# Weight units of 2048 columns split in one piece instead of two

## The chip, the cores and the metric

The kernel runs on one core of a Trainium2 chip. The metric is the device time of one execution in microseconds; three runs of the kernel before gave 905.27, 903.74 and 903.62, with a median of 903.74.

The engines of the core work side by side, each through its own list of instructions in order: TensorE (PE) multiplies matrices, ScalarE (ACT) and VectorE (DVE) work on elements, GpSimd (POOL) does a few odd things, and SyncE (SP) issues the transfers that bring the weights from HBM.

## The reference

Two layers of a hybrid encoder in float32, on 256 tokens of width 1024. One layer is, cut to what matters here:

```python
u = rms_norm(h, g_mix_pre)
gq, gk, gv, gg, ra_f, ra_b, aq, ak, av, gate_a, gate_b = split(u @ w_in)
a = (rms_norm(gla(forward) + gla(backward)) * silu(gg)) @ w_o_gla
b = gqa_attention(rope(rms_norm(aq)), rope(rms_norm(ak)), av) @ w_o_attn
h = h + rms_norm((sigmoid(gate_a) * a + sigmoid(gate_b) * b) @ w_out)
gate, up = split(rms_norm(h) @ w_ffn_in)
h = h + rms_norm((silu(gate) * up) @ w_ffn_out)
h = h + rms_norm(sigmoid(h @ w_ple_gate) * (p[i] @ w_ple_proj))
```

Nearly all the work is in the products with weights: `w_in`, `w_o_gla`, `w_o_attn`, `w_out`, `w_ffn_in`, `w_ffn_out`, `w_ple_gate` and `w_ple_proj`, each of which is read once per layer.

## The kernel before

**Products in three passes.** A float32 product is made of products of fp32r numbers. Each operand is split into a high part, the value rounded to fp32r, and a low part, the difference between the value and its high part. A product is then high by high, plus high by low, plus low by high. For the weights, `split` (L134 to L136) makes the high part `wh` with a copy on ACT and the low part `wl` with a subtract on DVE. The subtract reads what the copy wrote. `passes` (L116 to L124) issues the matmuls of a quarter of a product: for the four rows of 128 that a unit holds, first the eight matmuls that read only `wh` and then the four that read `wl` (with `fresh` both parts come earlier). The matmuls themselves are recorded at L108 (the helper `mm`) and L124 (`passes`).

**Units of weights.** All weights come as a stream of 176 units in a fixed order, listed by `plan` (L206 to L234). A unit is a 128x2048 block of float32 in SBUF: four blocks of 128 rows by 512 columns of a weight matrix, say. Eight units, those that also hold the decay ranks of `w_in`, are 2112 columns wide. `Load` and `Stream` (L236 to L367) carry them. `Stream.start` issues a unit's transfers on SP into a raw tile; there are three raw tiles. `Stream.fill` takes the next unit as soon as fewer than four are held. It calls `put`, which allocates the pair `wh` and `wl` (four of each) and cuts the unit into pieces; `fill` then calls `split` on each piece and asks for the next transfer. A raw tile comes free when the last subtract that reads it is done. `take` hands the oldest split unit to a product, and `done` gives its buffers back when the product is issued.

**Sums of units.** Part of the products over 2x2 blocks are done with seven block products instead of eight, on sums and differences of blocks. `Stream.step` (L324 to L346) forms the sums of weights with adds of 128x2048 on DVE (L328, L331, L334, L339) and puts each sum through `made`, which calls `put` and `split` too. In these the raw tiles are lent `wh` and `wl` tiles (`lent`) or larger scratch tiles (`big`).

**Order of the work.** A planner orders the instructions of each engine when the program is built, by priorities and its own estimate of times. What is within a block of high priority goes ahead when it is ready; `issue_after` pins one instruction behind another. On the chip each engine follows that order. `self.cast` and `self.last[n]` keep the instructions of the last piece of a unit, so that other instructions can be pinned behind it (`behind`, L357).

**Stages.** A layer runs through the keys and values of the GLA branch and the attention (`gqk`, `kv`, `rq`, `v`, `at`), the out-gate of the GLA branch (`gg`), the gates and merges of the branches (`gate`, `merge`), `wout`, the FFN (`ffnin`) and the input embedding (`ple`). Names of tiles in the profile carry the layer and the stage, so that `acc_0gate` is an accumulator in PSUM of the gate stage of layer 0.

**Transposes and gates.** The outputs of one product become the left operand of the next after a transpose. At the end of the FFN's first product they are transposed on PE (`transpose_in`, matmuls with the identity at L452) and split in turn, elsewhere by a DMA (`turn_out`, `take_in`, L458 to L484, with copies on ACT at L468 and L478). The FFN's gate is a silu on ACT (L1655) and a product on DVE (`vmul`, L129), which give the tile `t_0ffnin`.

Of the kernel before, what the change touches and what calls it, by code (L numbers as in the profile page):

```python
# [62 lines left out]
def trunk_kernel(ctx: ExitStack, tc: tile.TileContext, a: dict, out: bass.AP):  # L63
# [21 lines left out]
    def nm(s):  # L85
        uid[0] += 1
        return f"{s}_{part[0]}_{uid[0]}"
# [161 lines left out]
    class Stream:  # L249
# [51 lines left out]
                        on("dma", nc.sync.dma_start, dst, src)  # L301
                x.n = sum(math.prod(dst.shape[1:]) for dst, _ in moves)

        def put(self, x, parts=2):

            wh = wp.tile([P, UNIT], F32R, tag="wh", name=nm("wh"))
            wl = wp.tile([P, UNIT], F32R, tag="wl", name=nm("wl"))
            self.ready.append((wh, wl))
            self.held += 1
            cuts = [slice(j * x.n // parts, (j + 1) * x.n // parts) for j in range(parts)]  # L310
            return [(wh[:, c], wl[:, c], x.raw[:, c]) for c in cuts]
# [1494 lines left out]
```

## Time and profile before

| | |
|---|---|
| median of 3 runs | 903.74 us |
| lowest and highest run | 903.62 and 905.27 us |
| span of the profiled execution | 903.0 us |
| PE busy | 892.9 us in 4431 matmuls |
| DVE busy | 790.0 us in 1021 instructions |
| ACT busy | 641.4 us in 1035 instructions |
| read from and written to HBM | 169.50 and 3.15 MB |

The span is the time from the first to the last record of the profiled execution; the median of the runs is 0.7 us above it. Busy times are sums over an engine's instructions, with the profile's modelled ends for PE, so that an engine whose busy time is 99% of the span has nearly always an instruction under way. A row of the timeline gives the start in us, the length, the engine with the line of the kernel, the operation, what it writes and reads, the shape and how many such instructions are put together; in brackets stands the idle time before it and what ended that. A row of the groups gives the count, the busy time, the mean length of one in ns, and the idle time ahead of the group's instructions.

### The profile page before, as it was taken

How to read it: one execution, taken by the hardware profiler on the slowest of the kernel's cores; microseconds unless marked ns; L12 is line 12 of the kernel's file. 1: busy time of each engine (PE TensorE's matmuls, PEld its weight loads, DVE VectorE, ACT ScalarE, POOL GpSimd, SP SyncE). 2: the span in 40 equal slices, each digit the busy share in tenths (PEclk: the TensorE clock that was granted, in tenths of full speed). 3: DMA queues.
4: the chain of work that ended last, by engine and by line, in shares of the span. 5: the costliest groups of instructions: out<-in, count | busy, mean ns of one | idle time of the engine just before them, and what ended most of it. 6: DMA issues, size and time to landing. Idle time of an engine off the chain costs nothing.

```text
span 903.0 us, 12130 instructions
## 1 busy us (share of the span) xinstructions
PE 892.9 (99%) x4431; PEld 759.0 (84%) x4431; DVE 790.0 (87%) x1021; ACT 641.4 (71%) x1035; POOL 104.4 (12%) x157
## 2 busy tenths in 40 slices
PE   9999999999999999999999999999999999999996
PEld 8888888888888888888898888888888888888885
DVE  7899989997679999999779799899985799999984
ACT  6669769965468787766676697698645696967653
POOL 3800221000310000000234003210001100000001
PEclk9999999999999999999999999999999999999998
DMA  8764448469296695947476544473683966867441
GB/s 276 256 206 132 155 157 220 124 220 351 66 325 198 205 272 177 290 164 261 163 276 202 173 116 140 140 233 138 217 298 95 305 182 214 240 213 253 157 170 47
DMA packets 121191, 181.30 MB, mean 201 GB/s; under 512 B 35166, under 2 KB 59238, under 8 KB 120620
## 3 DMA queue, kind: packets, MB, share of 16 engines
q1 hardware_dynamic: 120972, 180.40, 61.5%
q8 instruction: 35, 0.57, 0.3%
q14 instruction: 24, 0.20, 0.1%
q10 hardware_dynamic: 160, 0.14, 0.0%
HBM read 169.50 MB, written 3.15 MB: 191 GB/s over the span
## 4 chain that ended last, share of the span: by engine, by line
PE 87%; DVE 6%; ACT 3%; issue 2%; DMA 1%; POOL 0%; POOLq 0%; ACTq 0%
PE acc_0ffnin L124 12%; PE acc_1ffnin L124 10%; PE acc_1gate L124 7%; PE acc_0gate L124 7%; PE acc_0ffnin L108 7%; PE acc_1ffnin L108 5%; PE acc_1rq L124 3%; PE acc_0wout L124 2%; PE acc_1wout L124 2%; PE acc_0ple L124 2%; PE acc_0gg L124 2%; PE acc_1gg L124 2%; PE acc_1merge L124 2%; PE acc_0merge L124 2%; PE acc_1ple L124 2%
## 5 line engine op out<-in xcount | busy, mean ns | idle before, releaser
L136 ACT CAST wh_0ffnin<-raw_0ffnin 128x1024 fp32r<-128x1024 f32 x38 | 38.6, 1049 | 19.6 <-PE acc_0ffnin L108 9.9
L136 ACT CAST wh_1ffnin<-raw_1ffnin 128x1024 fp32r<-128x1024 f32 x38 | 38.5, 1049 | 19.6 <-PE acc_1ffnin L108 9.8
L136 DVE TENSOR_TENSOR wl_1ffnin<-raw_1ffnin,wh_1ffnin 128x1024 fp32r<-128x1024 f32 x38 | 44.8, 1218 | 2.4 <-ACT wh_1ffnin L136 2.4
L136 DVE TENSOR_TENSOR wl_0ffnin<-raw_0ffnin,wh_0ffnin 128x1024 fp32r<-128x1024 f32 x38 | 44.8, 1219 | 2.3 <-ACT wh_0ffnin L136 2.3
L108 PE MATMUL acc_0ffnin<-wh_0ffnin,big_0ffnin 128*128 128x512 f32 x176 | 45.1, 390 | 0.0
L108 PE MATMUL acc_1ffnin<-wh_1ffnin,big_1ffnin 128*128 128x512 f32 x176 | 45.1, 390 | 0.0
L124 PE MATMUL acc_1ffnin<-wh_1ffnin,big_1wout 128*128 128x512 f32 x168 | 41.5, 389 | 0.0
L124 PE MATMUL acc_0ffnin<-wh_0ffnin,big_0wout 128*128 128x512 f32 x168 | 41.5, 389 | 0.0
L108 PEld LDWEIGHTS acc_1ffnin<-wh_1ffnin,big_1ffnin 128*128 128x128 f32 x176 | 33.0, 188 | 6.9
L108 PEld LDWEIGHTS acc_0ffnin<-wh_0ffnin,big_0ffnin 128*128 128x128 f32 x176 | 33.0, 188 | 6.9
L124 PEld LDWEIGHTS acc_1ffnin<-wh_1ffnin,big_1wout 128*128 128x128 f32 x168 | 31.5, 188 | 6.6
L124 PEld LDWEIGHTS acc_0ffnin<-wh_0ffnin,big_0wout 128*128 128x128 f32 x168 | 31.5, 188 | 6.6
L136 DVE TENSOR_TENSOR wl_0ffnin<-lent_0ffnin,wh_0ffnin 128x1024 fp32r<-128x1024 f32 x30 | 35.7, 1219 | 1.3 <-ACT wh_0ffnin L136 1.2
L136 DVE TENSOR_TENSOR wl_1ffnin<-lent_1ffnin,wh_1ffnin 128x1024 fp32r<-128x1024 f32 x30 | 35.7, 1220 | 1.1 <-ACT wh_1ffnin L136 0.9
L136 ACT CAST wh_1ffnin<-lent_1ffnin 128x1024 fp32r<-128x1024 f32 x30 | 30.4, 1052 | 6.7 <-DMA lent_1ffnin<-in_w_ffn_in_dram 3.4
L136 ACT CAST wh_0ffnin<-lent_0ffnin 128x1024 fp32r<-128x1024 f32 x30 | 30.4, 1051 | 6.3 <-DMA lent_0ffnin<-in_w_ffn_in_dram 2.9
L136 DVE TENSOR_TENSOR wl_0gate<-raw_0gate,wh_0gate 128x1024 fp32r<-128x1024 f32 x20 | 23.6, 1221 | 1.6 <-ACT wh_0gate L136 1.5
L136 DVE TENSOR_TENSOR wl_1gate<-raw_1gate,wh_1gate 128x1024 fp32r<-128x1024 f32 x20 | 23.6, 1219 | 1.6 <-ACT wh_1gate L136 1.5
L136 ACT CAST wh_0gate<-raw_0gate 128x1024 fp32r<-128x1024 f32 x20 | 20.1, 1048 | 6.5 <-PE acc_0gate L124 3.5
L136 ACT CAST wh_1gate<-raw_1gate 128x1024 fp32r<-128x1024 f32 x20 | 20.1, 1049 | 6.0 <-PE acc_1gate L124 3.5
L108 PE MATMUL acc_0ffnin<-wl_0ffnin,big_0ffnin 128*128 128x512 f32 x88 | 24.0, 391 | 0.0
L108 PE MATMUL acc_1ffnin<-wl_1ffnin,big_1ffnin 128*128 128x512 f32 x88 | 24.0, 391 | 0.0
(738 smaller groups left out, 2750.4 us busy)
## 6 DMA issues: line engine op xcount, KB each, us to landing
raw_0ffnin<-in_w_ffn_out_dram SPq DMA_DIRECT2D x11, 1024.0 KB, 5.4
raw_1ffnin<-in_w_ffn_out_dram SPq DMA_DIRECT2D x11, 1024.0 KB, 6.4
lent_0ffnin<-in_w_ffn_in_dram SPq DMA_DIRECT2D x6, 1024.0 KB, 7.5
lent_1ffnin<-in_w_ffn_in_dram SPq DMA_DIRECT2D x6, 1024.0 KB, 6.5
raw_0v<-in_w_in_dram SPq DMA_DIRECT2D x4, 1024.0 KB, 5.2
raw_0gate<-in_w_o_gla_dram SPq DMA_DIRECT2D x4, 1024.0 KB, 5.4
raw_0gate<-in_w_o_attn_dram SPq DMA_DIRECT2D x4, 1024.0 KB, 5.7
raw_0wout<-in_w_ffn_in_dram SPq DMA_DIRECT2D x8, 512.0 KB, 4.5
```

What stands on the lines that cost most here:

```text
L108: return nc.tensor.matmul(o, lhsT, rhs, start=start, stop=stop)
L124: nc.tensor.matmul(o, x, y, start=start and n == 0, stop=stop and n == len(seq) - 1, **kw)
L136: return nc.scalar.copy(hi, src), nc.vector.tensor_tensor(out=lo, in0=src, in1=hi.bitcast(F32), op=ALU.subtract)
```

## The change

`put` no longer takes the number of pieces as an argument. It chooses one piece where the unit has 2048 columns and two where it has another width. Both callers, `fill` and `made`, called it with two pieces; so each of the 168 units of 2048 columns gets one cast of 128x2048 and one subtract of 128x2048, where it had two of 128x1024 each. The eight units of 2112 columns keep two pieces of 1056. The tiles, the buffers, the transfers, the matmuls and their order in the program text are the same. The last piece of a unit, to which other instructions can be pinned, is then the whole unit. The first units of layer 0 that are split elsewhere in the start are not touched.

```diff
-        def put(self, x, parts=2):
-
+        def put(self, x):
+
+            parts = 1 if x.n == 2048 else 2
             wh = wp.tile([P, UNIT], F32R, tag="wh", name=nm("wh"))
             wl = wp.tile([P, UNIT], F32R, tag="wl", name=nm("wl"))
             self.ready.append((wh, wl))
```

## The prediction

> **What bounds the kernel now.** I read the page first (the head, the busy shares, the chain that ended last), then the waits of PE, then the windows.
>
> ```profile
> span 903.0 us, 12130 instructions
> PE 892.9 (99%) x4431; PEld 759.0 (84%) x4431; DVE 790.0 (87%) x1021; ACT 641.4 (71%) x1035; POOL 104.4 (12%) x157
> PE 87%; DVE 6%; ACT 3%; issue 2%; DMA 1%; POOL 0%; POOLq 0%; ACTq 0%
> ```
>
> ```profile
> PE warm L108 <- POOL seed L145: 1.0, 1, 1.0
> PE acc_0gqk L108 <- DVE big_0kv L136: 0.9, 1, 0.9
> PE aux_0at L108 <- DVE mid_0at L136: 0.6, 1, 0.6
> ```
>
> ```profile
> 0.00:10.00 10.00, 8.92 (x48) 1.00 0.80 256
> 10.00:880.00 870.00, 868.28 (x4293) 1.00 0.63 204
> ```
>
> PE is busy in 99% of the span and makes 87% of the chain. The waits view, which adds up idle time of PE by what ended it, has three entries, and the first is the start, which the change does not touch. The window row (length, then PE busy with its count, granted clock, DMA share, GB/s) says the same more sharply: from 10 to 880 us PE stands still for only 870.00 − 868.28 = 1.7 us. So this change, which touches ACT and DVE alone, can gain at most about 1.7 us inside the kernel. It can lose without such a limit: whatever makes a weight part arrive after PE wants it is added to the time. The question is therefore not how much busy time goes, but where PE now takes its operand just in time.
>
> **The prices.** A unit is 128x2048; each is now two casts on ACT (high part wh) and two subtracts on DVE (low part wl).
>
> ```profile
> L136 ACT CAST wh_0ffnin<-raw_0ffnin 128x1024 fp32r<-128x1024 f32 x38 | 38.6, 1049 | 19.6 <-PE acc_0ffnin L108 9.9
> L136 ACT CAST big_0ffnin<-mid_0ffnin 128x512 fp32r<-128x512 f32 x9 | 5.6, 619 | 0.1
> L136 DVE TENSOR_TENSOR wl_0ffnin<-raw_0ffnin,wh_0ffnin 128x1024 fp32r<-128x1024 f32 x38 | 44.8, 1219 | 2.3 <-ACT wh_0ffnin L136 2.3
> L334 DVE TENSOR_TENSOR lent_0ffnin<-lent_0ffnin,big_0ffnin 128x2048 f32<-128x2048 f32 x3 | 6.9, 2290 | 0.1
> ```
>
> Cast: from 512 to 1024 columns it grows by 1049 − 619 = 430 ns, 0.84 ns a column, so 2048 columns take 1049 + 860 = 1.91 us (an estimate by a straight line through two rows). Subtract: no subtract of 2048 columns is in the trace; an add of the same engine, form and width takes 2.29 us. It writes f32 where the subtract writes fp32r, and the bounds for that are the add itself and twice the 1024 row, 2.29 to 2.44 us; I take 2.29, since only the output's rounding differs.
>
> ```profile
> 164.84 2.00 ACT L136 CAST wh_0gate<-raw_0gate 128x1024 fp32r<-128x1024 f32 x2
> 165.93 2.36 DVE L136 TENSOR_TENSOR wl_0gate<-raw_0gate,wh_0gate 128x1024 fp32r<-128x1024 f32 x2
> ```
>
> A back-to-back pair overlaps a little: 2.00 us on ACT, 2.36 us on DVE (timeline: start, us, instruction, count). So **what is removed** is 0.09 us of ACT and 0.06 us of DVE a unit; over the 168 units that change (176 less the 8 that are 2112 wide) it is 15 us of ACT and 10 us of DVE. Neither engine bounds the kernel, so by itself that is worth nothing outside the 1.7 us. **What is added** is a wait. In the rows above the first subtract starts 1.09 us after the first cast began, and the low part is whole at 168.29, that is 3.45 us after the cast's start. Merged, the subtract cannot start before the whole cast is done: 1.91 + 2.29 = 4.20 us. Where DVE is free when the cast begins, the low part comes 0.75 us later (0.82 by the usual pair of 2.35); where DVE has a queue longer than the cast, it comes 0.06 us sooner. A second cost: an urgent small DVE instruction behind a weight subtract waits for up to 2.29 us instead of 1.22. Nothing is removed from or added to the DMA queue, but a raw buffer is freed when its subtract ends, so that loads that wait for a buffer move by the same amounts.
>
> **Gate stage (acc_gate, by the first merge of the branches), both layers.** Units are split ahead of their use, and a later low part is hidden wherever that lead is over 0.8 us. Following PE's order through the timeline, this stage is the first place where it is not.
>
> ```profile
> 148.72 1.05 ACT L136 CAST wh_0gate<-lent_0gate 128x1024 fp32r<-128x1024 f32 x1
> 151.57 1.05 ACT L136 CAST wh_0gate<-lent_0gate 128x1024 fp32r<-128x1024 f32 x1
> 154.19 2.00 ACT L136 CAST wh_0gate<-raw_0gate 128x1024 fp32r<-128x1024 f32 x2
> 159.28 1.99 ACT L136 CAST wh_0gate<-big_0gate 128x1024 fp32r<-128x1024 f32 x2
> 162.30 2.35 DVE L136 TENSOR_TENSOR wl_0gate<-big_0gate,wh_0gate 128x1024 fp32r<-128x1024 f32 x2
> 164.57 1.29 DVE L136 TENSOR_TENSOR big_0gg<-big_0gg,big_0gg 128x512 fp32r<-128x512 f32 x2
> 164.36 0.57 ACT L742 COPY mid_0gate<-acc_0gate 128x512 f32<-128x512 f32 x1
> 166.40 1.98 PE L124 MATMUL acc_0gate<-wh_0gate,big_0gg 128*128 128x512 f32 x8
> 168.21 1.07 PE L124 MATMUL acc_0gate<-wl_0gate,big_0gg 128*128 128x512 f32 x4
> ```
>
> ```profile
> 150.00:160.00 10.00, 10.00 (x46) 8.29 (x45) 10.00 (x11) 10.00 (x13) 0.00 (x0) 1.00 1.00 206
> ```
>
> ACT (the fourth busy figure of that window row, after PE, PEld and DVE) has no idle time, so three earlier merged casts bring this one forward by 3 × 0.09 = 0.27: it runs from 164.57 to 166.48. DVE is done with the work before it at 165.86 (164.57 + 1.29), so the subtract runs when the cast is done, 166.48 to 168.77. PE wants wl at 168.21: 0.56 us late. (Now its first half is there at 167.11, 1.1 us early.) The eight matmuls on wh ahead of it do not save it: wh is whole at 166.48, and they start at 166.40. PE has 0.08 us of that wait anyway, which is the same wait and not counted twice.
>
> ```profile
> 614.52 2.00 ACT L136 CAST wh_1gate<-raw_1gate 128x1024 fp32r<-128x1024 f32 x2
> 617.88 1.07 PE L124 MATMUL acc_1gate<-wl_1gate,big_1gg 128*128 128x512 f32 x4
> ```
>
> In layer 1 cast and use are 3.36 us apart, as in layer 0 (3.37). Term: 2 × 0.56 = **+1.1 us**.
>
> **End of the FFN, both layers.**
>
> ```profile
> 405.04 3.90 ACT L136 CAST wh_0ffnin<-raw_0ffnin 128x1024 fp32r<-128x1024 f32 x4 [3.73 <-PE acc_0ffnin L108]
> 406.23 4.63 DVE L136 TENSOR_TENSOR wl_0ffnin<-raw_0ffnin,wh_0ffnin 128x1024 fp32r<-128x1024 f32 x4
> 410.77 0.68 DVE L129 TENSOR_TENSOR t_0ffnin<-mid_0ffnin,t_0ffnin 128x512 f32<-128x512 f32 x1
> 411.65 0.60 PE L452 MATMUL aux_0ffnin<-ident,t_0ffnin 128*128 128x128 f32 x4
> 408.61 5.51 SPq L299 DMA_DIRECT2D raw_0ffnin<-in_w_ple_gate_dram  x3
> 413.74 2.00 ACT L136 CAST wh_0ffnin<-raw_0ffnin 128x1024 fp32r<-128x1024 f32 x2 [0.87 <-DMA raw_0ffnin<-in_w_ple_gate_dram]
> 414.84 1.22 DVE L136 TENSOR_TENSOR wl_0ffnin<-raw_0ffnin,wh_0ffnin 128x1024 fp32r<-128x1024 f32 x1
> 416.31 0.69 DVE L129 TENSOR_TENSOR t_0ffnin<-mid_0ffnin,t_0ffnin 128x512 f32<-128x512 f32 x1 [0.25 <-ACT t_0ffnin L1655]
> 417.05 0.42 PEld L452 LDWEIGHTS aux_0ffnin<-ident,t_0ffnin 128*128 128x128 f32 x4 [0.44 <-DVE t_0ffnin L129]
> ```
>
> ACT was idle for 3.73 us and begins two units when PE frees their buffers; DVE follows. Merged: the cast ends at 405.04 + 1.91 = 406.95, the subtracts run 406.95 to 409.24 and 409.15 to 411.44, and the gate product t behind them starts at 411.35 instead of 410.77, 0.58 later. PE's transposes of t have 411.65 − 411.45 = 0.2 to spare, so they come about 0.4 late: 2 × 0.4 = **+0.8 us**.
>
> The first subtract pair ends at 406.23 + 2.35 = 408.58 and frees the buffer into which the load at 408.61 goes. Merged it ends at 409.24, so the load, and the cast at 413.74 that waits for it, come 0.65 later: the cast runs 414.39 to 416.30. The silu that t waits for stands behind that cast, so t starts at 416.9 instead of 416.31 and PE's second transposes, which already wait for t (the 0.44 in the PEld row), come 0.6 late, 0.2 of it beyond the 0.4 that PE has lost before: 2 × 0.2 = **+0.4 us**, if t still goes ahead of the whole subtract. If it goes behind it (subtract 416.31 to 418.60), that is a case below.
>
> ```profile
> 855.43 0.60 PE L452 MATMUL aux_1ffnin<-ident,t_1ffnin 128*128 128x128 f32 x4
> 860.95 0.66 PE L452 MATMUL aux_1ffnin<-ident,t_1ffnin 128*128 128x128 f32 x4
> ```
>
> In layer 1 both steps stand at nearly the same distance (5.52 us; 5.40 in layer 0), so each term counts twice.
>
> **Attention stage.** Here small urgent splits stand between the weight subtracts.
>
> ```profile
> 500.73 0.36 ACT L136 CAST big_1kv<-aux_1kv 128x256 fp32r<-128x256 f32 x1
> 504.86 0.41 DVE L136 TENSOR_TENSOR big_1kv<-aux_1kv,big_1kv 128x256 fp32r<-128x256 f32 x1
> 505.06 1.14 PE L108 MATMUL aux_1at<-big_1kv,mid_1at 128*128 128x256 f32 x7
> ```
>
> The split of 504.86 ends at about the time when PE begins (0.2 us), so a later one is paid in full; its chain begins with an urgent cast at 500.73 which now stands between two casts of a unit, and would stand behind one that is 0.86 us longer. In layer 0 the two waits of 0.9 and 0.6 us stand at the same kind of split. Bounds: if DVE's queue is full there, each is 0.06 to 0.3 sooner, −0.5 in all; if an urgent split falls behind a longer subtract, 2.29 − 1.22 = 1.07 later each at two places, and 0.4 for the rest, +2.5. I take **+0.5**, nearer the bottom, because most urgent splits in these rows stand directly before a subtract and not behind one.
>
> **Sum.** 1.1 + 0.8 + 0.4 + 0.5 = +2.8 us on the profiled execution's 903.0 us of span. The median of the runs, 903.74, is 0.7 above that span, which I take to be what lies around it and unchanged: **906.5 us**.
>
> **The rivals.**
>
> *The second transposes of the FFN stand behind the whole subtract.* DVE's order is fixed when the program is built, and t is ready 0.5 us after the subtract could start. Then t starts at 418.5 and PE is 2.2 late per layer instead of 0.6: 906.5 + 2 × 1.6 = 909.7. For it: the subtract is ready first. Against it: in the rows of before t was put between two subtracts though the second was ready. It decides wherever the builder expects t later than the cast's end. Chance 0.20, 908.5 to 911.
>
> *Not slower: the builder moves PE's order.* The late things are few, and each stands beside products whose operands are ready. If the transposes are placed some matmuls later (each matmul is 0.22 us, so three cover the 0.6), and the gate product of 168.21 gets its cast ahead of the copy of 0.57 us at 164.36, no term is left: 903.7, from 902.9 to 904.5. The point from which it decides is 0.6 us of other ready PE work at each of the four places. Against it: the gate stage has one product after the other, with the unit as its next operand. Chance 0.25.
>
> *Faster: the shorter queues count.* If the splits behind PE's waits of 0.9 and 0.6 come sooner by the freed DVE and ACT time and nothing else is late, 903.74 − 1.5 = 902.2; all the idle time from 10 to 880 us is 1.7. Chance 0.08, about 0.05 of it below 901.93. The Trainium skill, "Perfetto Trace Analysis", section "Optimizing Scalar/DVE Operations", says that grouping into larger operations can improve throughput if the engine is saturated, which speaks for this case; in the same place it says that where Scalar and Vector are not saturated but cause bubbles on other engines, breaking instructions up may let work be completed sooner, which speaks against the change. By the trace DVE at 87% and ACT at 71% are on the second side, and the rows of 405.04 and 164.84 with it.
>
> *The change does nothing:* excluded but for the condition; units of another width than 2048 keep two pieces, and the form rows would show it (0.01, inside the case of 903.7).
>
> **How the numbers follow.** Forecast 0.45 (905.0 to 907.8), the second transposes 0.20, covered 0.25, faster 0.08, something worse 0.02. The range that leaves out less than 2 in 10, with the bounds of the attention stage: 902.0 to 911.0. About 0.2% (1.8 us) is what a measurement can tell from no change, so the limits are 901.93 and 905.55. Slower: 0.45 less 0.08 that falls below 905.55, and 0.20 and 0.02, 0.59. Faster: 0.05. Same: 0.08 + 0.25 + 0.03 = 0.36.
>
> **What would show it.** Casts of 128x2048 at 1.91 us and subtracts at 2.29, 168 of each in place of 336. DVE at about 780 us and ACT at 626, with PE's busy time as it was. New idle time of about 0.5 us on PE before the wl matmuls that stand at 168.21 and 617.88 now, and before the transposes at 411.65, 417.06 and their twins of layer 1; PE's idle from 10 to 880 us up from 1.7 to 4.5. The prediction is wrong if those places show no wait, if casts or subtracts of 2048 columns cost other than the rows say, or if the order of PE's matmuls differs so much that stages no longer match one to one.

## The result

The changed kernel takes 914.01 us (median of 4 runs, 913.62 to 916.28), the kernel before 903.75 (median of 4, 903.62 to 905.27). The ratio is 1.0111, with a 95% interval from 1.0099 to 1.0122: slower by 10.3 us. The forecast was 906.5, with a range to 911.0. The direction was right, the size was not.

The page of the changed kernel, its head and its chain:

```profile
span 912.1 us, 11769 instructions
PE 896.2 (98%) x4431; PEld 756.6 (83%) x4431; DVE 776.9 (85%) x853; ACT 627.7 (69%) x867; POOL 121.3 (13%) x157
PE 81%; ACT 7%; DVE 5%; issue 3%; POOL 2%; DMA 1%; SPq 0%; POOLq 0%; ACTq 0%; DVEq 0%
```

There are 168 fewer instructions on ACT and on DVE, which have 13.7 and 13.1 us less to do. POOL has the same 157 instructions and 16.9 us more (104.4 before). It was not in the prediction's sum at all, and it is in the chain now with 2%, where it had 0%.

Two of the merged groups of the FFN, in the groups view:

```profile
L136 ACT CAST wh_0ffnin<-raw_0ffnin 128x2048 fp32r<-128x2048 f32 x19 | 36.2, 1915 | 21.5 <-PE acc_0ffnin L108 7.1
L136 DVE TENSOR_TENSOR wl_0ffnin<-raw_0ffnin,wh_0ffnin 128x2048 fp32r<-128x2048 f32 x19 | 43.4, 2288 | 4.8 <-ACT wh_0ffnin L136 4.8
```

1915 and 2288 ns: the prices were right to 5 ns. What PE waits for is in the waits view of the changed kernel:

```profile
PE aux_0wout L453 <- DVE mid_0wout L547: 0.9, 1, 0.9
PE aux_0at L124 <- DVE mid_0at L136: 0.9, 1, 0.9
PE aux_1at L124 <- DVE mid_1at L136: 0.9, 1, 0.9
PE aux_1wout L453 <- DVE mid_1wout L547: 0.8, 1, 0.8
PE acc_1gate L124 <- ACT wh_1gate L136: 0.7, 1, 0.7
PE aux_0at L108 <- DVE mid_0at L136: 0.7, 1, 0.7
PE acc_0gate L124 <- ACT wh_0gate L136: 0.7, 1, 0.7
PE aux_0at L108 <- ACT big_0kv L136: 0.6, 1, 0.6
```

and the window from 10 to 880 us, in which PE stood still for 1.7 us before:

```profile
10.00:880.00 870.00, 862.80 (x4246) 1.00 0.64 204
```

Now it stands still for 7.2 us there. These are waits of under 1 us, one a place, the same places in both layers: gate, wout, attention.

**Where the time was lost.** Both traces hold 4431 matmuls. The start of the n-th matmul in one, less that of the n-th in the other, is how far PE has fallen behind, and its growth over a stretch is what that stretch lost (us, worked out from the two traces in that way; a stretch is named by its end on the clock of the kernel before):

| stretch | to 10.5 | attention and GLA, to 154 | gates, to 241 | wout, to 250 | FFN, to 406 | its tail and embedding, to 448 | layer 1: attention, to 601 | gates, to 690 | wout, to 706 | FFN, to 851 | tail, to 895 |
|---|---|---|---|---|---|---|---|---|---|---|---|
| changed | -0.81 | 1.08 | 2.07 | 1.33 | 0.00 | 1.12 | 0.68 | 2.03 | 1.33 | 0.00 | 0.23 |

Together 9.06, near the difference of the spans, 9.1 (912.1 - 903.0). The first 10 us are no part of the change: nearly all runs below are 0.4 to 1.2 us ahead there, so it was the profiled execution of before that began late. Without them the loss is 9.9 us, near the 10.3 of the medians. The two FFN stretches, about a third of each layer, with 75 of the 168 changed units, lost nothing. Gates and wout lost 6.8, the same in both layers.

**The wout stage.** Timeline of before, the norm between the mixer and the FFN (ACT's cast and second sum of squares, DVE's first subtract and the scaling `mid`, POOL's add on 128x1, PE's transposes):

```profile
240.20 1.03 ACT L136 CAST wh_0wout<-raw_0merge 128x1024 fp32r<-128x1024 f32 x1
241.14 0.63 ACT L526 ACTIVATE t_0wout<-h 128x512 f32<-128x512 f32 x1
241.27 1.23 DVE L136 TENSOR_TENSOR wl_0wout<-raw_0merge,wh_0wout 128x1024 fp32r<-128x1024 f32 x1 [1.07 <-ACT wh_0wout L136]
243.35 1.42 DVE L546 SCALAR_TENSOR_TENSOR mid_0wout<-h,rstd_0wout,mid_0merge 128x512 f32<-128x512 f32 x2 [0.86 <-POOL rstd_0wout L542]
241.96 0.70 POOL L538 TENSOR_SCALAR rstd_0wout<-ss_0wout 128x1 f32<-128x1 f32 x1 [3.21 <-ACT t_0wout L526]
245.09 1.03 PE L452 MATMUL aux_0wout<-ident,mid_0wout 128*128 128x128 f32 x8
```

The same in the changed kernel:

```profile
242.53 1.89 ACT L136 CAST wh_0wout<-raw_0merge 128x2048 fp32r<-128x2048 f32 x1
244.33 0.63 ACT L527 ACTIVATE t_0wout<-h 128x512 f32<-128x512 f32 x1
244.46 2.29 DVE L136 TENSOR_TENSOR wl_0wout<-raw_0merge,wh_0wout 128x2048 fp32r<-128x2048 f32 x1 [1.93 <-ACT wh_0wout L136]
247.60 1.42 DVE L547 SCALAR_TENSOR_TENSOR mid_0wout<-h,rstd_0wout,mid_0merge 128x512 f32<-128x512 f32 x2 [0.85 <-POOL rstd_0wout L543]
245.14 1.77 POOL L539 TENSOR_SCALAR rstd_0wout<-ss_0wout 128x1 f32<-128x1 f32 x1 [4.06 <-ACT t_0wout L527]
248.50 1.29 PE L453 MATMUL aux_0wout<-ident,mid_0wout 128*128 128x128 f32 x8 [0.92 <-DVE mid_0wout L547]
```

Two waits stand one behind the other. First, the sum of squares is behind the whole cast instead of its first half (1.89 - 1.03 = 0.86 later). Second, POOL's add on 128 numbers takes 1.77 us instead of 0.70, 1.07 more. It is not slow: it ends at 246.91, 0.16 after the DVE subtract that was running when it began (244.46 + 2.29 = 246.75), and in the kernel before it ended 0.16 after its subtract too (242.66 against 242.50). DVE then stands idle for 0.85 us until POOL is done, PE 0.92.

### The profile page after: what moved, and what is told of

The parts are those of the page before. It is cut to its first block, busy times and chain, and to the rows that moved or that the text cites. A ratio compares the mean times of both kernels' runs of the same rounds, so it can differ in the third digit from the quotient of the medians.

```text
span 912.1 us, 11769 instructions
## 1 busy us (share of the span) xinstructions
PE 896.2 (98%) x4431; PEld 756.6 (83%) x4431; DVE 776.9 (85%) x853; ACT 627.7 (69%) x867; POOL 121.3 (13%) x157
## 4 chain that ended last, share of the span: by engine, by line
PE 81%; ACT 7%; DVE 5%; issue 3%; POOL 2%; DMA 1%; SPq 0%; POOLq 0%; ACTq 0%; DVEq 0%
PE acc_1ffnin L124 12%; PE acc_0ffnin L124 12%; PE acc_1ffnin L108 7%; PE acc_0ffnin L108 6%; PE acc_0gate L124 4%; PE acc_1gate L124 4%; PE acc_1rq L124 3%; PE acc_1merge L124 2%; PE acc_0merge L124 2%; PE acc_0gqk L108 2%; PE acc_1ple L124 2%; PE acc_0gg L124 2%; PE acc_1gg L124 2%; PE acc_0wout L124 2%; PE acc_1wout L124 2%
## 5 line engine op out<-in xcount | busy, mean ns | idle before, releaser
L136 ACT CAST wh_0ffnin<-raw_0ffnin 128x2048 fp32r<-128x2048 f32 x19 | 36.2, 1915 | 21.5 <-PE acc_0ffnin L108 7.1
L136 ACT CAST wh_1ffnin<-raw_1ffnin 128x2048 fp32r<-128x2048 f32 x19 | 36.2, 1913 | 20.0 <-PE acc_1ffnin L108 7.3
L136 DVE TENSOR_TENSOR wl_1ffnin<-raw_1ffnin,wh_1ffnin 128x2048 fp32r<-128x2048 f32 x19 | 43.4, 2289 | 4.8 <-ACT wh_1ffnin L136 4.8
L136 DVE TENSOR_TENSOR wl_0ffnin<-raw_0ffnin,wh_0ffnin 128x2048 fp32r<-128x2048 f32 x19 | 43.4, 2288 | 4.8 <-ACT wh_0ffnin L136 4.8
L136 ACT CAST wh_1ffnin<-lent_1ffnin 128x2048 fp32r<-128x2048 f32 x15 | 28.8, 1918 | 12.0 <-PE acc_1ffnin L124 5.2
L136 DVE TENSOR_TENSOR wl_1ffnin<-lent_1ffnin,wh_1ffnin 128x2048 fp32r<-128x2048 f32 x15 | 34.3, 2290 | 3.0 <-ACT wh_1ffnin L136 3.0
L136 DVE TENSOR_TENSOR wl_0ffnin<-lent_0ffnin,wh_0ffnin 128x2048 fp32r<-128x2048 f32 x15 | 34.2, 2288 | 2.1 <-ACT wh_0ffnin L136 2.1
L136 ACT CAST wh_0ffnin<-lent_0ffnin 128x2048 fp32r<-128x2048 f32 x15 | 28.8, 1919 | 9.8 <-PE acc_0ffnin L124 5.2
L136 DVE TENSOR_TENSOR wl_1gate<-raw_1gate,wh_1gate 128x2048 fp32r<-128x2048 f32 x10 | 22.8, 2289 | 4.0 <-ACT wh_1gate L136 4.0
L136 DVE TENSOR_TENSOR wl_0gate<-raw_0gate,wh_0gate 128x2048 fp32r<-128x2048 f32 x10 | 22.8, 2288 | 2.1 <-ACT wh_0gate L136 2.1
```

The source lines that it names most:

```text
L136: return nc.scalar.copy(hi, src), nc.vector.tensor_tensor(out=lo, in0=src, in1=hi.bitcast(F32), op=ALU.subtract)
```

## The experiments

Three theories of one cause stood at first: A, the long cast blocks ACT; D, the long subtract blocks DVE and POOL; F, the low part is late because its subtract waits for the whole cast. Beside them stood the question whether the loss sits at the places that the table shows, or comes from another order of all instructions.

All kernels are the changed one with one thing altered; `unit` is a unit's place in its layer, counted from 0. Medians of 4 to 6 runs stand beside those of the kernel before (4 to 12 runs) on the same chip. The losses by stretch are got as above, against the trace of before:

| kernel | median, before, ratio (interval) | attention 0 | gates 0 | wout 0 | tail 0 | attention 1 | gates 1 | wout 1 | FFN 1 | tail 1 |
|---|---|---|---|---|---|---|---|---|---|---|
| changed | 914.01, 903.75, 1.0111 (1.0099-1.0122) | 1.08 | 2.07 | 1.33 | 1.12 | 0.68 | 2.03 | 1.33 | 0.00 | 0.23 |
| cast1_sub2 | 914.88, 904.10, 1.0115 (1.0097-1.0133) | 2.63 | 1.73 | 0.27 | 0.63 | 0.63 | 1.72 | 0.28 | 1.49 | 0.55 |
| cast2_sub1 | 912.92, 904.10, 1.0100 (1.0085-1.0115) | 1.29 | 2.09 | 0.00 | -0.05 | 0.61 | 2.04 | 0.00 | 1.24 | 0.10 |
| gate_two | 912.29, 904.10, 1.0098 (1.0081-1.0115) | 1.21 | 1.21 | 1.34 | 1.49 | 0.63 | 1.23 | 1.34 | 0.00 | 0.15 |
| wout_two | 912.08, 904.10, 1.0089 (1.0074-1.0104) | 1.08 | 2.06 | 0.00 | 0.95 | 0.71 | 2.07 | 0.00 | 0.75 | 0.16 |
| early_two | 911.11, 903.63, 1.0083 (1.0070-1.0095) | 1.06 | 0.82 | 1.33 | 0.74 | 0.66 | 0.77 | 1.33 | 0.00 | 0.19 |
| merge_two | 911.81, 903.63, 1.0088 (1.0075-1.0101) | 1.05 | 0.91 | 1.33 | 1.20 | 0.69 | 0.91 | 1.34 | 0.00 | 0.18 |
| v_two | 912.91, 903.63, 1.0103 (1.0090-1.0116) | 1.18 | 1.99 | 1.33 | 0.99 | -0.25 | 2.02 | 1.33 | 0.00 | 0.17 |
| tight_two | 907.36, 903.63, 1.0035 (1.0023-1.0047) | 0.23 | 0.03 | 0.00 | 0.74 | -0.17 | 0.00 | 0.00 | 0.00 | 0.78 |
| ten_two | 908.95, 903.94, 1.0049 (1.0035-1.0063) | 1.20 | 0.00 | 0.00 | 1.41 | -0.16 | -0.01 | 0.00 | 0.51 | 0.18 |
| ffn_one | 906.48, 904.24, 1.0028 (1.0017-1.0039) | 0.48 | 0.00 | 0.00 | 0.48 | 0.00 | 0.00 | 0.00 | 0.29 | 0.52 |
| att_four | 908.18, 904.24, 1.0038 (1.0025-1.0051) | 2.54 | 0.03 | 0.00 | 0.00 | 0.22 | 0.00 | 0.00 | 1.18 | 0.57 |
| all_four | 908.73, 904.24, 1.0044 (1.0033-1.0056) | 0.95 | 0.26 | 0.00 | 0.04 | 0.49 | 0.22 | 0.00 | 0.07 | 0.21 |

(The FFN of layer 0 lost 0.00, but 0.75 in cast1_sub2, 0.25 in cast2_sub1, 0.11 in ten_two, 0.32 in ffn_one and 0.34 in all_four.)

### One half of the merge alone

Both diffs are cut to the case of 2048 columns; `hs` are its two halves.

```diff
-        return nc.scalar.copy(hi, src), nc.vector.tensor_tensor(out=lo, in0=src, in1=hi.bitcast(F32), op=ALU.subtract)
+        cast = nc.scalar.copy(hi, src)
+        subs = [nc.vector.tensor_tensor(out=lo[:, c], in0=src[:, c], in1=hi[:, c].bitcast(F32), op=ALU.subtract) for c in hs]
+        return cast, subs[-1]
```

> Cast of a unit of 2048 columns in one piece as in the changed kernel, the subtract in two pieces of 1024. Theory D (the loss comes from a subtract of 2.29 us on DVE that cannot be interrupted: urgent DVE instructions and POOL's small ones that share SBUF with it wait for its end): most of the loss goes, 904 to 907 us, and POOL's 128x1 add that took 1.77 us in the wout stage of layer 0 is back at 1.2 or less. Theory A (a cast of 1.91 us blocks ACT): the loss stays, 912 to 914. Theory F (the low part is late because the subtract waits for the whole cast): the first low half still comes 0.8 us later than before, so over half of the loss stays, 909 to 911.

```diff
+        casts = [nc.scalar.copy(hi[:, c], src[:, c]) for c in hs]
+        return casts[-1], nc.vector.tensor_tensor(out=lo, in0=src, in1=hi.bitcast(F32), op=ALU.subtract)
```

> Casts in two pieces of 1024 as before the change, the subtract in one piece of 2048. Theory D: the loss stays, 912 to 915 us. Theory A: it goes, 904 to 906. Theory F: it stays, 912 to 914, since the low part is whole only 4.3 us after the cast's start. D and F part at POOL: D expects its 128x1 adds of the wout stage at 1.7 to 2.1 us as in the changed kernel.

Neither half is the cause by itself: each alone costs about as much as both, at partly other places. D had 904 to 907 for the first kernel, F 909 to 911, and it took 914.88; A had 904 to 906 for the second, and it took 912.92. So all three theories of one cause fell. In the wout stage, where ACT and POOL keep their order, the two can be read apart. DVE and POOL there, with the whole cast and two subtracts:

```profile
246.71 1.22 DVE L139 TENSOR_TENSOR wl_0wout<-raw_0merge,wh_0wout 128x1024 fp32r<-128x1024 f32 x1 [1.92 <-ACT wh_0wout L138]
247.40 0.70 POOL L544 TENSOR_SCALAR rstd_0wout<-ss_0wout 128x1 f32<-128x1 f32 x1 [4.06 <-ACT t_0wout L532]
```

and with two casts and the whole subtract:

```profile
247.23 4.49 DVE L141 TENSOR_TENSOR wl_0wout<-raw_0merge,wh_0wout 128x2048 fp32r<-128x2048 f32 x2
244.91 0.30 POOL L544 TENSOR_SCALAR rstd_0wout<-ss_0wout 128x1 f32<-128x1 f32 x1 [3.21 <-ACT t_0wout L532]
```

The first has the late sum of squares and POOL's add at 0.70, and loses 0.27 us. In the second the subtract can only start after both casts and was put behind the norm, POOL meets no subtract (0.30), and nothing is lost. For the changed kernel the sum goes: `mid` came 0.86 + 1.07 = 1.93 later. Before, PE's transposes began 1.74 us after the start of `mid` (245.09 against 243.35); with the wait it is 0.90, so 0.84 of it was slack. 1.93 - 0.84 = 1.09, and 0.26 more for the eight transposes (1.29 us from the first to the last instead of 1.03): 1.35 against 1.33 measured. With the late sum alone, 0.86 - 0.84 + 0.26 = 0.28 against 0.27. D's expectation for the second kernel's POOL adds (1.7 to 2.1 us) held only for a later one in each layer, which took 1.96.

### Two pieces again at one place

The line of the change, with the units that are in two pieces again; `gate_two` has (20, 21, 22, 23, 24), `wout_two` (41, 42, 43), `early_two` (17, 18, 19, 20), `merge_two` (24,), `v_two` (13,):

```diff
-            parts = 1 if x.n == 2048 else 2
+            unit = self.total - len(self.jobs) - 1
+            parts = 1 if x.n == 2048 and unit % 89 not in (20, 21, 22, 23, 24) else 2
```

> The changed kernel, with two pieces again only for the five units of each layer that are split last ahead of the first merges (units 20 to 24 of a layer), 10 units in all. If the loss is local, the 2.0 us that each layer's gate stage lost come back: about 910 us. Rival (the builder's order differs everywhere and the places are only where it shows): less than 1.5 us come back, 912.5 or more.

> The changed kernel, with two pieces again only for the three units of each layer that are split while the norm between the mixer and the FFN is formed (units 41 to 43 of a layer), 6 units in all. If the loss is local, PE's wait of 0.9 us before the transposes of mid_wout goes in both layers and 1.4 us each come back: about 911.3 us, with POOL's second 128x1 add at 0.7 us instead of 1.77. Rival (another load of DVE takes the place): less than 1 us comes back, 913 or more.

> The changed kernel, with two pieces again for units 17 to 20 of each layer only, which are split 15 to 45 us ahead of the place in the gate stage where PE waits. Theory O (most of the gate stage's loss, 1.2 of 2.0 us a layer, is ACT's queue: the casts of the sums on mid_gate were moved behind, because whole units were put ahead of them): about 1.2 us a layer comes back in that stage, 2.4 in all. Rival (the loss is the lateness of unit 24's own high and low parts): nothing comes back there.

> The changed kernel, with two pieces again for unit 24 of each layer only, the unit at which PE waits in the gate stage. If its own lateness counts: 0.8 us a layer comes back in that stage, as when units 20 to 24 were in two pieces, since PE can begin with the first half of wh; 1.2 us a layer stay, from ACT's later queue. Rival (the queue alone): less than 0.3 us a layer comes back.

> The changed kernel, with two pieces again for unit 13 of each layer only. Its two subtracts stood on both sides of the urgent split of mid_at; the whole one was put ahead of it. Theory D: PE's wait of 0.9 us for mid_at goes in both layers and 0.8 us a layer comes back in the attention stage. Rival (that wait comes from other units' casts): less than 0.3 a layer.

**wout_two** brings both losses of 1.33 to 0.00, and POOL's add is back at 0.71; 0.75 are given back right behind it in layer 1, where PE now waits 0.5 us for the second half of `mid_1wout`. **v_two** takes layer 1's attention from 0.68 to -0.25. Its cause is the order, as these rows of DVE and PE show; first the changed kernel:

```profile
536.98 2.29 DVE L136 TENSOR_TENSOR wl_1v<-raw_1gqk,wh_1v 128x2048 fp32r<-128x2048 f32 x1
542.33 1.28 DVE L136 TENSOR_TENSOR mid_1at<-aux_1at,mid_1at 128x512 fp32r<-128x512 f32 x2
543.07 0.50 PE L124 MATMUL aux_1at<-mid_1at,big_1kv 128*128 128x512 f32 x1 [0.85 <-DVE mid_1at L136]
```

and with unit 13 in two pieces:

```profile
535.10 1.21 DVE L136 TENSOR_TENSOR wl_1v<-raw_1gqk,wh_1v 128x1024 fp32r<-128x1024 f32 x1
539.98 1.28 DVE L136 TENSOR_TENSOR mid_1at<-aux_1at,mid_1at 128x512 fp32r<-128x512 f32 x2
541.18 2.28 DVE L136 TENSOR_TENSOR wl_1v<-raw_1gqk,wh_1v 128x2048 fp32r<-128x2048 f32 x1
```

In the changed kernel the whole subtract of unit 14 (536.98) stands ahead of the end of the chain that makes `mid_1at`. With unit 13 in two pieces, its second half (535.10) stands there, and the whole subtract of unit 14 comes behind the chain (541.18). So the length of one unit moved the place of the next one. The expectation had the units wrong: in the kernel before it is unit 14, not 13, whose two subtracts (530.99 and 537.07) stand on both sides of that chain. In layer 0 PE's wait for `mid_0at` at 87.53 fell from 0.86 to 0.10 us as well, but a wait of 0.52 came at 101.63, where the changed kernel has none, and the stage still lost 1.18.

**The gates** are two losses. The changed kernel, ACT, DVE and PE:

```profile
139.41 0.64 ACT L136 CAST mid_0gate<-mid_0gate 128x512 fp32r<-128x512 f32 x1
146.75 1.05 ACT L469 COPY big_0gg<-mid_0gg 128x1024 uint16<-128x1024 uint16 x1 [2.90 <-DVE mid_0gg L129]
147.71 1.14 ACT L136 CAST mid_0gate<-mid_0gate 128x512 fp32r<-128x512 f32 x2
166.05 1.91 ACT L136 CAST wh_0gate<-raw_0gate 128x2048 fp32r<-128x2048 f32 x1
168.02 2.11 PE L124 MATMUL acc_0gate<-wh_0gate,big_0gg 128*128 128x512 f32 x8 [0.65 <-ACT wh_0gate L136]
170.34 1.21 PE L124 MATMUL acc_0gate<-wl_0gate,big_0gg 128*128 128x512 f32 x4 [0.21 <-DVE wl_0gate L136]
```

and early_two, in which only units 17 to 20, long ahead of that place, are in two pieces again:

```profile
134.90 0.62 ACT L136 CAST mid_0gate<-mid_0gate 128x512 fp32r<-128x512 f32 x1 [1.67 <-DVE mid_0gate L129]
143.11 1.69 ACT L136 CAST mid_0gate<-mid_0gate 128x512 fp32r<-128x512 f32 x3
146.81 2.00 ACT L470 COPY big_0gg<-mid_0gg 128x1024 uint16<-128x1024 uint16 x2 [2.02 <-DVE mid_0gg L129]
164.56 1.91 ACT L136 CAST wh_0gate<-raw_0gate 128x2048 fp32r<-128x2048 f32 x1
168.85 1.21 PE L124 MATMUL acc_0gate<-wl_0gate,big_0gg 128*128 128x512 f32 x4 [0.19 <-DVE wl_0gate L136]
```

With whole units the first cast of the sums `mid_0gate` is at 139.41 instead of 134.90, and the other three come when ACT's busy stretch has begun (from 147.71) instead of ahead of it, at 143.11, when ACT had time. So each later cast of that stretch is late, that of unit 24 by 1.49 us (166.05 against 164.56); 0.25 of that is not the stage's own, as PE came into it 0.27 us late in one trace (1.08 - 0.81) and 0.02 in the other. That is the greater part: 2.07 - 0.82 = 1.25 us a layer go when the order is back. What then stays, 0.82, is unit 24's own lateness. merge_two takes 1.16 of the 2.07, more than the 0.8 expected, by letting PE begin on the first half of unit 24: with 1.25 that is more than 2.07, so an early first half hides part of the queue's delay too. gate_two, with units 20 to 24 in two pieces, took 0.86 and 0.80 where 2.0 was expected; the casts of the sums stayed late there (139.46 and from 146.77). With both changes (ten_two) nothing is left.

### The places together, and the rest alone

tight_two: the tuple is units 5 to 24, 41 to 44 and 80 to 87. ten_two: 13, 17 to 20, 24, 41 to 44. ffn_one turns it round (`unit` is taken modulo 89 ahead of this line):

```diff
+            parts = 1 if x.n == 2048 and 46 <= unit <= 76 else 2
```

> The changed kernel, with two pieces again for units 5 to 24, 41 to 44 and 80 to 87 of each layer; the other units of 2048 columns, 104 in all, above all the FFN's, stay in one piece. If the loss lies in the places named, it is gone: 903 to 905 us, no slower than the kernel before. Rival (the longer pieces cost everywhere a little): 906 or more.

> The changed kernel, with two pieces again for ten units of each layer only (13, 17 to 20, 24 and 41 to 44), the ones at the places that single runs have shown; the other 148 stay in one piece. If those places add up: the gate stages' 2.0, the wout stages' 1.3 and the second layer's attention's 0.8 us come back, some 7.5 us of the 10, and 906 to 907.5 is left. Rival (the builder puts the wait elsewhere when these go): 909 or more.

> One piece only for units 46 to 76 of each layer, the middle of the FFN, where DVE's and ACT's work is weights alone and every unit is split long ahead; 62 of the 168 units. All others in two pieces. If one piece costs only where something waits: within 1 us of the kernel before, 903 to 904.7. Rival (the longer pieces cost a little wherever they stand): 905 or more.

In tight_two 105 units stay whole (ACT has 930 instructions there, 867 in the changed kernel), and the loss falls from 10.3 us to 3.7. With ten units a layer (ten_two) it falls to 5.0, and gates, wout and layer 1's attention lose nothing. Neither gets to the forecast (903 to 905 and 906 to 907.5), and ffn_one says why the rule "whole pieces are free where weights are the only work" is too simple: 62 whole units in the middle of the FFN, and 2.2 us slower than before. Its losses in the trace are 0.3 to 0.5 us in five stretches. One of these is the attention of layer 0, ahead of its first whole unit, so half a microsecond in one stretch is about what such a comparison of two traces can't tell from nothing; both FFNs and their tails are the others. By the trace ffn_one lost 2.1 us without the first 10 us, tight_two 1.6 and ten_two 3.2, while their medians are 2.2, 3.7 and 5.0 above before. The trace is of one run, in tight_two and ten_two one of the fastest of theirs; the same holds for all_four below, which lost 2.6 by the trace and 4.5 by the medians. What the other runs lost more isn't shown.

### More pieces instead of fewer

```diff
+            parts = 4 if x.n == 2048 and 4 <= unit <= 17 else 2
```

all_four has `parts = 4 if x.n == 2048 else 2`.

> The other direction: four pieces of 512 columns for units 4 to 17 of each layer, which are split during the attention stage, two pieces for the rest. Theory D: urgent splits and POOL's small instructions wait less, PE's waits of 0.9 and 0.6 us in layer 0 shrink, 902.0 to 903.2 us. Rival (those waits come from the order or from the latency of the chain itself): 903.5 or more, since each further piece adds 0.1 us of ACT and 0.06 us of DVE.

> Four pieces of 512 columns for all units of 2048. Theory D: as with four pieces in the attention stage, with the gate stage's queue on ACT longer by 0.2 us a unit, 902 to 904 us. Rival (the fixed cost of a piece decides where ACT and DVE have no idle time): 905 or more.

Four pieces are slower too, by 3.9 and 4.5 us, so a shorter piece is no cure in itself and theory D fails here. The rows of att_four, DVE and PE:

```profile
53.04 3.69 DVE L136 TENSOR_TENSOR wl_0kv<-raw_0rq,wh_0kv 128x512 fp32r<-128x512 f32 x6
56.65 0.75 DVE L136 TENSOR_TENSOR big_0kv<-aux_0kv,big_0kv 128x256 fp32r<-128x256 f32 x2
57.12 0.73 PE L108 MATMUL acc_0gqk<-big_start,wh_0kv 128*128 128x512 f32 x2 [1.86 <-DVE big_0kv L136]
```

Six short subtracts of weights stand in a row ahead of the split that PE waits 1.86 us for (0.88 before). Whether some of them could have gone behind it, and where the rest of the 2.54 us of that stage went, was not tested. No kernel here is faster than the one before.

## Why the prediction was wrong

Two steps failed above all: at the gates the prediction took ACT's order to stay as it was, and in wout its list of what a longer instruction holds up left out the norm. Together they are 5.7 of the 7.1 us that the sum was short.

- **The bound** was right: PE is the bound, it had 1.7 us to give, and what was freed on ACT and DVE (13.7 and 13.1 us; forecast 15 and 10) made no kernel faster.
- **The prices** were right: 1915 and 2288 ns for 1.91 and 2.29 us. (The 0.82 beside the 0.75 does not come out of its rows: 4.20 - 1.09 - 2.35 is 0.76. No term rests on it.)
- **Gates**, 2 x 0.56 forecast, 2.07 and 2.03 measured. The step that failed is the one that took ACT's order from the trace of before and moved unit 24's cast *forward* by 0.27. In the changed kernel it began 1.2 us later (166.05 against 164.84; 0.9 beside PE, which was 0.27 late there), because the casts of the sums were put behind. With that order back (early_two) the step is nearly exact: cast forecast at 164.57, measured 164.56; the wl matmuls forecast 0.56 late, so 168.77, measured 168.85; the loss 0.82 and 0.77, with 0.2 of it not in the sum.
- **wout** had no term and cost 1.33 twice. The step that failed is the list of what a longer instruction holds up: the prediction named "an urgent small DVE instruction behind a weight subtract", and neither the sum of squares behind a longer cast on ACT nor POOL's small instructions, which wait for the subtract's end as well. The rows of before had the second: the 128x1 add at 241.96 took 0.70 us while the same form took 0.30 elsewhere.
- **The FFN's end**, 0.6 a layer forecast. The tails lost 1.12 and 0.23, 1.35 for 1.2, but that the sums agree is luck: the step that failed is the one that kept PE's order. In the changed kernel the transposes stand six matmuls later in PE's list than before (14 at the second place of layer 1) and wait 0.03 us at most, as these rows show, the first place of layer 0 and the second of layer 1:

```profile
416.11 0.69 DVE L129 TENSOR_TENSOR t_0ffnin<-mid_0ffnin,t_0ffnin 128x512 f32<-128x512 f32 x1
416.85 0.66 PE L453 MATMUL aux_0ffnin<-ident,t_0ffnin 128*128 128x128 f32 x4
870.18 2.29 DVE L136 TENSOR_TENSOR wl_1ffnin<-raw_1ffnin,wh_1ffnin 128x2048 fp32r<-128x2048 f32 x1 [1.02 <-ACT wh_1ffnin L136]
872.39 0.69 DVE L129 TENSOR_TENSOR t_1ffnin<-mid_1ffnin,t_1ffnin 128x512 f32<-128x512 f32 x1
873.13 0.66 PE L453 MATMUL aux_1ffnin<-ident,t_1ffnin 128*128 128x128 f32 x4
```

About 0.2 us a layer went there, instead of 0.6. That is the mechanism of the rival "Not slower", at this one stage. Layer 0 lost 0.44 more at the transposes of `h` right behind (`aux_0ffnout`) and 0.47 at a wait for the next layer's embedding input, and there was no term for either. Of the rival of 909.7 the condition was met in layer 1, where the second t stands behind the whole subtract (870.18, then 872.39), and not in layer 0, where t starts at 421.54 and the subtract follows at 422.15. Its price of 2.2 us was not paid even in layer 1, as the transposes stand later as well.
- **Attention**, 0.5 forecast, 1.08 and 0.68 measured: inside its bounds (up to 2.5), on the upper side. Against the reason given, a whole subtract was put ahead of the urgent chain in layer 1 (v_two).
- **The time**: 9.9 us without the start, against 2.8 forecast. Of the 7.1 between them 3.0 are at the gates (4.1 for 1.1), 2.7 at wout, 1.3 in attention (1.8 for 0.5) and 0.1 at the tail. "The median is 0.7 above the span" was off too: other runs show 1.7 to 1.8, so the profiled execution of before was itself about 1 us slower than the median, most likely in its first 10 us.

The faster rival's condition, freed time that shortens PE's waits while nothing else is late, was not met. Of the two waits in layer 0's attention the one of 0.62 us at 101.58 did go, but that of 0.88 at 56.48 became two, 0.63 for `big_0kv` and 0.66 for `mid_0at`, and a new one of 0.86 for `mid_0at` came at 87.53.

## What to carry to other kernels

When the bound engine has under 0.2% of idle time, price a longer instruction on the others by what stands behind it, on every engine that shares something with it, and not by its fixed cost saved: here 168 merges saved 27 us of engine time and cost 10. Where a builder fixes the order, pieces are also what it orders by, so a change of size everywhere is a change of order everywhere: widen the range by what one such swap costs at each place with little slack (here 0.7 to 1.3 us). Here both fewer and more pieces than two were slower, so try a change of the number at one place before all.

## What the runs showed of the hardware

POOL's small instructions wait for the DVE subtract that runs beside them. The group rows of before and of the changed kernel, the same instructions on 128 numbers:

```profile
L532 POOL TENSOR_SCALAR ss_0wout<-ss_0wout 128x1 f32<-128x1 f32 x1 | 0.3, 302 | 5.0 <-ACT t_0wout L526 5.0
L589 POOL TENSOR_SCALAR rs_0ple<-ss_0ple 128x1 f32<-128x1 f32 x2 | 5.6, 2790 | 4.2 <-ACT t_0ple L586 4.2
```

```profile
L533 POOL TENSOR_SCALAR ss_0wout<-ss_0wout 128x1 f32<-128x1 f32 x1 | 2.1, 2092 | 5.1 <-ACT t_0wout L527 5.1
L590 POOL TENSOR_SCALAR rs_0ple<-ss_0ple 128x1 f32<-128x1 f32 x2 | 11.7, 5832 | 4.9 <-ACT t_0ple L587 4.9
```

302 ns became 2092, and one of the two `rs_0ple` took 8.09 us (4.01 before), through several DVE instructions in a row. Most of those that began inside a whole subtract of weights ended 0.13 to 0.17 us after it. What the DVE instruction reads decides: the 302 ns of before also fell inside a DVE subtract, `big_0wout<-aux_0wout,big_0wout` (248.09, 0.68 us), but one of its two inputs, the product `aux_0wout`, lies in PSUM. In the 14 traces together, from 30 us on, 118 of POOL's `TENSOR_SCALAR` instructions on 128x1 began inside a DVE `TENSOR_TENSOR` with an input in PSUM, and none took over 0.34 us.

The Trainium skill, "SBUF — State Buffer", section "Who interferes with whom", says that a DVE instruction with two SBUF inputs contends with a GpSimd instruction that reads SBUF, and that the ports they share are an exclusive lock; these rows agree. The 8.09 us suggest that the waiting one need not get its turn after a single DVE instruction.
